# Hybrid encoder layer, attention stage: sample units that hold both key heads, a fourth probability buffer, and turns and values one round later

## The chip, the cores and the metric

The kernel runs on one core of a Trainium2 chip: a TensorE (PE) for matmuls, a VectorE (DVE), a ScalarE (ACT), a GpSimd (POOL), and DMA queues. The metric is the device time of one execution in microseconds, the median of three runs. A round, below, is one turn of the loop over attention units; a step is one piece of other matmul work put between them.

## The reference, cut to what matters

The layer runs over 1024 prompt rows and 8 samples of 16 new rows each. Ahead of the part shown stand a SwiGLU and one input projection, behind it an output projection and a second SwiGLU.

```python
def sink_attention(q, k, v, bias, sinks, mask=None):
    s = jnp.einsum('...qhgd,...khd->...hgqk', q, k) * (HEAD_DIM ** -0.5) + bias
    ...
    sink_col = jnp.broadcast_to(sink, s.shape[:-1] + (1,))
    p = jax.nn.softmax(jnp.concatenate([s, sink_col], axis=-1), axis=-1)[..., :-1]
    return jnp.einsum('...hgqk,...khd->...qhgd', p.astype(v.dtype), v)
...
attn, gm, state = mixer(q, k, v, u, vn)
merged = jax.nn.sigmoid(ga) * (attn @ w_ba) + jax.nn.sigmoid(gb) * (gm @ w_bg)
```

There are 16 query heads over 2 key heads, 64 wide. A prompt query sees its own chunk of 64 keys and the two before it; a sample's 16 queries see 128 cached keys and the 16 new ones.

## The kernel before

The rows stand in 9 tiles of 128: block 0 holds five prompt tiles, block 1 three prompt tiles and one tile of the 8 samples. Large matmuls are made of three (`mm3`, L254 to L256) from operands that are split into a high and a low part (L264 on ACT and L265 on DVE for activations, L157 and L160 for weights).

`attend` runs a block's attention. Its units are in a fixed order: for each of eight pairs of query heads every prompt tile of the block (40 units in block 0, 24 in block 1), and in block 1 then 16 sample units, one for each key head and sample. A unit has four stages. *Scores*: matmuls (L1202; L1270 and L1271 for samples), bias and row bound on DVE (L1205; L1273), exponentials on ACT (L1210; L1278), into a buffer `pb`. *Divide*: on DVE, sum, reciprocal and product in `pb` (L1225, or L1229 for the first tile; L1286 for samples). *Turn*: PE transposes the probabilities (L1237; L1291), and one copy takes them out of PSUM into `pt` (L1238, alternating between DVE and ACT; L1292 on DVE). *Values*: matmuls with the values (L1250; L1301), and after the last unit of a group a copy into `attn_f` (L1254; L1306).

Round u divides unit u-2, scores unit u, turns unit u-2 and forms the values of unit u-3; there are three prompt buffers `pb`. After the scores and after the turn come steps of `second()`, the filler: six matmuls of the gMLP branch (L254 to L256), 64 in all, ten of them ahead of the first unit, and a rate such that some stay over for the end. `strict` keeps each engine's instructions in the order in which they are written, so an instruction that waits holds up all behind it on its engine.

A sample unit uses 64 rows of the array for its scores and 64 columns for its values; GpSimd clears its part of `pb` (L1267). The last unit of a key head copies all its heads' outputs (L1306). When the attention is done, `put_split` splits each of the eight `attn_f` tiles (L264, L265), with a step of the filler in between, and `first()` multiplies them by `w_ba`; later on the same stretch the norms and transposes of the next stage follow (L332 on DVE, L435 on PE).

Of the kernel before, what the change touches and what calls it, by code (L numbers as in the profile page):

```python
# [27 lines left out]
P = 128  # L28
# [13 lines left out]
def tile_hybrid_layer(  # L42
# [827 lines left out]
    k_smp = place(52, P)  # L870
    q_smp = place(28).rearrange("p (b a q) -> p b a q", b=8, a=8)
    k_c = [place(32 + 2 * i, 512).rearrange("p (b j) -> p b j", b=4) for i in range(2)]
# [33 lines left out]
    class Block:  # L906
# [44 lines left out]
        def project(self, tasks):  # L951
# [3 lines left out]
            rs_t, rs_s = (place(kb, 512).rearrange("p (g i) -> p g i", g=4) for kb in (56, 58))  # L955
# [37 lines left out]
            def row_sums():  # L993

                ones = tmp(P)
                nc.gpsimd.memset(ones, 1.0)
                for out, wt in ((rs_t, ws_t), (rs_s, ws_s))[:1 + b]:
                    ps = bank().rearrange("p (g i) -> p g i", g=4)
                    nc.tensor.matmul(ps, ones, wt, start=True, stop=True)
                    nc.scalar.copy(out=out, in_=ps)  # L1000
# [75 lines left out]
            def done(g, m, c, j, v, in_place):  # L1076
# [33 lines left out]
                else:  # L1110
                    hp = slice(64 * (f // 4), 64 * (f // 4) + 64)
                    for e in range(2):
# [5 lines left out]
                        if n_pr < w:  # L1118
                            nc.scalar.activation(out=q_smp[hp, :, 2 * (f % 4) + e, :],
# [20 lines left out]
        def attention(self):  # L1140
            self.pb = [wide() for _ in range(3)]
# [6 lines left out]
            if self.b == 1:  # L1148
                units += [(self.sample_unit, (h, i)) for h in range(2) for i in range(8)]
            return units  # L1150

        def keys(self, h):
# [8 lines left out]
            if h == 1:  # L1161
                t = wr.tile([P, 2048], F32, tag="wr", name="wr")[:, :320 * self.n_k]
                nc.gpsimd.memset(t, 0.0)
                self.vz = t.rearrange("p (m c) -> p m c", c=320)
            nc.scalar.copy(out=self.vz[:, :, 64 + 128 * h:128 + 128 * h],
                           in_=v_t[:, self.t0:self.t0 + self.n_k, mine])
# [11 lines left out]
        def prompt_unit(self, p, mi, u):  # L1178
            m = self.tiles[mi]
            h = p // 4  # L1180
            pb = self.pb[u % 3]
# [50 lines left out]
            def turn():  # L1232
# [5 lines left out]
                (nc.vector.tensor_copy if u % 2 else nc.scalar.copy)(out=pt[:, a0:], in_=ps[:, a0:])  # L1238

            def values():  # L1240
# [6 lines left out]
                for a in range(a0, 2):  # L1247
                    for e in range(2):
                        at = 64 + 128 * h - 64 * e
                        nc.tensor.matmul(po[:, c0:c0 + P], self.vz[:, m - 1 - self.t0 + a, at:at + P],  # L1250
# [7 lines left out]
        def sample_unit(self, h, i, u):  # L1258
            hp = slice(64 * h, 64 * h + 64)
            pb = self.pb[u // 2 % 3][:, u % 2 * 256:u % 2 * 256 + 256]  # L1260
            pt = place(53, 768)[:, u % 3 * 256:u % 3 * 256 + 256].rearrange("p (a t) -> p a t", a=2)
            new = pb[:, P + 16 * i:P + 16 * i + 16]
            s = stat()
            sink = sink_s[:, h:h + 1]

            def scores():
                nc.gpsimd.memset(pb[:, P:256], 0.0)  # L1267
# [4 lines left out]
                sc = tmp(144)  # L1272
                nc.vector.tensor_tensor_reduce(out=sc, in0=ps[:, 0:144], in1=bs_s[:, h], scale=1.0,  # L1273
                                               scalar=nsink_s[:, h:h + 1], op0=ALU.add, op1=ALU.min,
                                               accum_out=s[:, 2:3])
                nm = s[:, 2:3]
                for v, src, c in ((pb[:, 0:P], sc[:, 0:P], 4), (new, sc[:, P:144], 5)):
                    nc.scalar.activation(out=v, in_=src, func=AF.Exp, bias=nm, scale=-1.0,  # L1278
                                         accum_out=s[:, c:c + 1])
                nc.scalar.activation(out=s[:, 6:7], in_=nm, func=AF.Exp, bias=sink)  # L1280

            def divide():
                nc.vector.scalar_tensor_tensor(out=s[:, 8:9], in0=s[:, 4:5], scalar=s[:, 5:6],
                                               in1=s[:, 6:7], op0=ALU.add, op1=ALU.add)
                nc.vector.reciprocal(out=s[:, 10:11], in_=s[:, 8:9])
                nc.vector.tensor_scalar(out=pb, in0=pb, scalar1=s[:, 10:11], scalar2=None, op0=ALU.mult)  # L1286

            def turn():
                ps = bank()[:, 0:256].rearrange("p (a t) -> p a t", a=2)
                for a in range(2):  # L1290
                    nc.tensor.transpose(ps[:, a, :], pb[:, a * P:(a + 1) * P], ident)  # L1291
                nc.vector.tensor_copy(out=pt, in_=ps)  # L1292

            def values():
                if i == 0:
                    self.out[8 + h] = bank()
                po = self.out[8 + h]
                rw = pt.rearrange("p a (g e q) -> p a g e q", g=4, e=2)
# [159 lines left out]
    dn = {}  # L1458
# [172 lines left out]
```

## Time and profile before

| | us |
|---|---|
| three runs | 2608.41, 2610.66, 2612.6 |
| median | 2610.66 |
| profiled execution, its own time | 2607.29 |
| its span, first to last instruction | 2605.3 |
| block 0's attention, in the span | 1104 to 1230 |
| block 1's attention | 1584 to 1720, its sample units from 1662 |

The span is 2 us under the profiled execution's time, which is 3.4 us under the median. The two attentions are a tenth of the span; nearly all of the rest is the projections and SwiGLUs. Times in the rows below are microseconds from the start of the span. In a timeline row the bracket at the end gives the idle time before the instruction and what ended it; PEclk is the granted TensorE clock as a share of 2.4 GHz.

### The profile page before, as it was taken

The numbers are of one execution on the slowest core, as the hardware profiler recorded it, in microseconds if no ns is written. First come the engines' busy times: TensorE is split into PE (matmuls) and PEld (weight loads), VectorE is DVE, ScalarE is ACT, GpSimd is POOL, SyncE is SP. The second block draws the span as 40 slices with busy tenths as digits, with TensorE's granted clock in tenths as the row PEclk, the third lists the DMA queues.
The fourth block names the chain that finished last, engine by engine and source line by source line (L and its number), as shares of the span: only waits on it lengthen the run. The fifth ranks groups of instructions, "written<-read, shape, count | busy, mean of one in ns | idle before, by whom it ended". The sixth has DMA issues, their size and how long they took to land.

```text
span 2605.3 us, 43435 instructions
## 1 busy us (share of the span) xinstructions
PE 2534.7 (97%) x16996; PEld 2375.2 (91%) x16996; DVE 1902.0 (73%) x3312; ACT 1392.3 (53%) x2589; POOL 197.3 (8%) x302
## 2 busy tenths in 40 slices
PE   6999999999999999999999998899999999999998
PEld 6999987999978999989989898897999987899986
DVE  6776664788877686687867877778876665688885
ACT  5444553555565555775446567535544464455552
POOL 1000000000210000101300201141000000000030
PEclk9999999999999999999999999989999999999999
DMA  4423322333443224423533443353322323433362
GB/s 123 95 84 97 114 80 96 129 115 101 162 146 116 80 92 134 129 89 128 174 110 98 142 149 112 108 193 132 114 82 90 98 81 109 126 102 111 128 210 81
DMA packets 222476, 303.35 MB, mean 116 GB/s; under 512 B 11848, under 2 KB 174000, under 8 KB 222272
## 3 DMA queue, kind: packets, MB, share of 16 engines
q1 hardware_dynamic: 183312, 212.36, 25.5%
q0 software_dynamic: 19584, 64.08, 8.1%
q10 hardware_dynamic: 19376, 24.15, 2.6%
q8 instruction: 133, 2.18, 0.4%
q14 instruction: 71, 0.58, 0.1%
HBM read 260.43 MB, written 40.11 MB: 115 GB/s over the span
## 4 chain that ended last, share of the span: by engine, by line
PE 88%; DVE 7%; DMA 2%; ACT 1%; issue 1%; ACTq 0%; DVEq 0%; SPq 0%
PE ps L254 27%; PE ps L256 27%; PE ps L255 27%; PE ps L1250 1%; DVE wl L160 1%; PE ps L435 1%; DMA wr<-in_ffn_w_up_dram 1%; PE ps L1237 1%; DMA wr<-in_w_in_dram 1%; DVE arena_r L265 1%; PE ps L1202 1%; DVE arena_r L1176 1%; PE ps L1050 0%; DMA y<-w 0%; DVE w L1205 0%
## 5 line engine op out<-in xcount | busy, mean ns | idle before, releaser
L254 PE MATMUL ps<-arena_r,wh 128*128 128x320 f32 (+1 forms) x4160 | 1243.8, 299 | 3.9 <-ACT arena_r L264 1.4
L256 PE MATMUL ps<-arena_r,wl 128*128 128x320 f32 (+1 forms) x4160 | 1229.2, 296 | 4.9 <-DVE wl L160 4.6
L255 PE MATMUL ps<-arena_r,wh 128*128 128x320 f32 (+1 forms) x4160 | 1230.5, 296 | 0.4 <-DVE arena_r L265 0.3
L254 PEld LDWEIGHTS ps<-arena_r,wh 128*128 128x128 f32 x4160 | 788.1, 189 | 7.0 <-ACT arena_r L264 1.7
L256 PEld LDWEIGHTS ps<-arena_r,wl 128*128 128x128 f32 x4160 | 786.9, 189 | 7.0 <-DVE wl L160 6.8
L255 PEld LDWEIGHTS ps<-arena_r,wh 128*128 128x128 f32 x4160 | 788.4, 190 | 1.9 <-DVE arena_r L265 0.8
L160 DVE TENSOR_TENSOR wl<-wr,wh 128x1024 fp32r<-128x1024 f32 x404 | 503.5, 1247 | 248.0 <-ACT wh L157 239.0
L157 ACT CAST wh<-wr 128x1024 fp32r<-128x1024 f32 x404 | 419.7, 1039 | 211.2 <-PE ps L255 168.8
L254 PE MATMUL ps<-wh,arena_r 128*128 128x512 f32 x936 | 375.7, 401 | 1.0 <-ACT arena_r L264 1.0
L256 PE MATMUL ps<-wh,arena_r 128*128 128x512 f32 x936 | 371.4, 397 | 0.4 <-DVE arena_r L265 0.4
L255 PE MATMUL ps<-wl,arena_r 128*128 128x512 f32 x936 | 369.3, 395 | 0.0
L264 ACT CAST arena_r<-arena 128x640 fp32r<-128x640 f32 (+4 forms) x260 | 167.8, 654 | 267.7 <-PE ps L255 224.4
L265 DVE TENSOR_TENSOR arena_r<-arena,arena_r 128x640 fp32r<-128x640 f32 (+4 forms) x260 | 197.2, 768 | 147.9 <-ACT arena_r L264 142.6
L256 PEld LDWEIGHTS ps<-wh,arena_r 128*128 128x128 f32 x936 | 176.1, 188 | 43.4 <-DVE arena_r L265 0.8
L255 PEld LDWEIGHTS ps<-wl,arena_r 128*128 128x128 f32 x936 | 176.3, 188 | 40.8
L254 PEld LDWEIGHTS ps<-wh,arena_r 128*128 128x128 f32 x936 | 176.2, 188 | 40.9 <-ACT arena_r L264 1.9
L541 DVE TENSOR_TENSOR t<-t,ps 128x320 f32<-128x320 f32 (+1 forms) x384 | 169.9, 448 | 44.9 <-PE ps L256 34.9
L160 DVE TENSOR_TENSOR wl<-arena,wh 128x1024 fp32r<-128x1024 f32 (+1 forms) x130 | 156.7, 1205 | 56.0 <-ACT wh L157 55.5
L545 ACT COPY t<-ps 128x320 f32<-128x320 f32 (+1 forms) x384 | 150.9, 395 | 80.8 <-PE ps L256 80.0
L157 ACT CAST wh<-arena 128x1024 fp32r<-128x1024 f32 (+1 forms) x130 | 134.6, 1036 | 109.0 <-PE ps L255 87.2
L597 ACT ACTIVATE t<-t 128x256 f32<-128x256 f32 (+1 forms) x129 | 57.2, 444 | 173.9 <-DVE t L541 173.8
L157 ACT CAST wh<-gn 128x1024 fp32r<-128x1024 f32 (+1 forms) x65 | 67.5, 1039 | 51.0 <-PE ps L255 42.1
(248 smaller groups left out, 2215.9 us busy)
## 6 DMA issues: line engine op xcount, KB each, us to landing
wr<-in_ffn_w_gate_dram SPq DMA_DIRECT2D x88, 512.0 KB, 4.0
wr<-in_ffn_w_up_dram SPq DMA_DIRECT2D x88, 512.0 KB, 5.0
wr<-in_w_in_dram SPq DMA_DIRECT2D x84, 512.0 KB, 4.8
wr<-in_ffn_w_down_dram SPq DMA_DIRECT2D x40, 1024.0 KB, 5.1
y<-w ACTq DMA_DIRECT2D x38, 256.0 KB, 3.4
arena<-x POOLq DMA_DIRECT2D x19, 512.0 KB, 4.5
arena<-y POOLq DMA_DIRECT2D x17, 512.0 KB, 4.9
x<-arena POOLq DMA_DIRECT2D x16, 512.0 KB, 3.0
```

The source lines that it names most:

```text
L157: nc.scalar.copy(out=self.hi, in_=self.src)
L160: nc.vector.tensor_tensor(out=self.lo, in0=self.src, in1=self.hi.bitcast(F32), op=ALU.subtract)
L254: nc.tensor.matmul(out, lh, rh, start=start, stop=False, skip_group_check=again)
L255: nc.tensor.matmul(out, lh, rl, start=False, stop=False, skip_group_check=again)
L256: nc.tensor.matmul(out, ll, rh, start=False, stop=stop, skip_group_check=again)
L264: nc.scalar.copy(out=hi, in_=src)
L265: nc.vector.tensor_tensor(out=lo, in0=src, in1=hi.bitcast(F32), op=ALU.subtract)
L435: nc.tensor.transpose(ps[:, c0:c0 + n], self.h[self.tiles[i]][p0:p0 + n, k * P:(k + 1) * P], ident[p0:p0 + n, p0:p0 + n])
L541: nc.vector.tensor_tensor(out=out, in0=a, in1=b, op=ALU.add)
L545: nc.scalar.copy(out=t, in_=ps)
L597: nc.scalar.activation(out=t, in_=v, func=AF.Silu)
L1176: nc.vector.tensor_tensor(out=t[other], in0=src, in1=t[mine].bitcast(F32), op=ALU.subtract)
```

## The change

A sample unit now holds both key heads. The queries of key head h lie in a tile of their own whose other 64 rows are zeros, so scores are matmuls over all 128 rows; the new values of each sample lie in the first 16 rows of a zeroed tile; eight units of four score matmuls, four transposes and two values matmuls of 256 columns replace sixteen. Every second unit copies two samples' outputs for all heads in four copies.

`pb` has four buffers (the fourth in the tile that also holds `vz`, the values among zeros, made narrower). Divide stays two rounds behind the scores; turn is three behind and values four. Three copies of four out of the turns go to ACT. The cached keys are copied by ACT in three instructions, where DVE needed eight.

```diff
@@ attention
-            self.pb = [wide() for _ in range(3)]
+            room = wr.tile([P, 2048], F32, tag="wr", name="wr")
+            self.vz = room[:, :256 * self.n_k + 64]
+            nc.gpsimd.memset(self.vz, 0.0)
+            self.pb = [wide() for _ in range(3)] + [room[:, 1536:2048]]
...
-                units += [(self.sample_unit, (h, i)) for h in range(2) for i in range(8)]
+                units += [(self.sample_unit, (i,)) for i in range(8)]
@@ prompt_unit, turn
-                (nc.vector.tensor_copy if u % 2 else nc.scalar.copy)(out=pt[:, a0:], in_=ps[:, a0:])
+                (nc.vector.tensor_copy if u % 4 == 3 else nc.scalar.copy)(out=pt[:, a0:], in_=ps[:, a0:])
@@ sample_unit
-                lq = q_smp[hp, i].rearrange("p a q -> p (a q)")
-                nc.tensor.matmul(ps[:, 0:P], lq, k_c[i // 4][hp, i % 4, :], start=True, stop=True)
-                nc.tensor.matmul(ps[:, P:P + 16], lq, k_smp[hp, 16 * i:16 * i + 16], start=True, stop=True)
+                if i < 4:
+                    nc.gpsimd.memset(pb[:, :, 144:256], 0.0)
...
+                for h in range(2):
+                    lq = q_smp[h][:, i].rearrange("p a q -> p (a q)")
+                    for c, k in ((0, k_c[:, i, :]), (P, k_smp[:, 16 * i:16 * i + 16])):
+                        nc.tensor.matmul(ps[:, 144 * h + c:144 * h + c + k.shape[-1]], lq, k, start=True, stop=True)
...
-                nc.vector.tensor_copy(out=pt, in_=ps)
+                nc.scalar.copy(out=pt, in_=ps)
...
-                for a, vv in ((0, v_c[:, i, hp]), (1, v_smp[:, hp])):
-                    for e in range(2):
-                        nc.tensor.matmul(po[64 * e:64 * e + 64, i * 64:(i + 1) * 64], vv,
-                                         rw[:, a, :, e, :], start=(a == 0), stop=(a == 1))
-                if i == 7:
...
+                for a, vv in ((0, v_c[:, i, :]), (1, v_new[i // 4][:, i % 4, :])):
+                    nc.tensor.matmul(po[:, i % 2 * 256:i % 2 * 256 + 256], vv, pt[:, a, :], start=a == 0, stop=a == 1)
+                if i % 2:
...
+                    for h in range(2):
+                        for e in range(2):
+                            (nc.vector.tensor_copy if e else nc.scalar.copy)(
...
@@ attend
-            lag = [[None] * 4] * 3
-            for u, (kind, arg) in enumerate(units + [(None, None)] * 3):
...
-                for i, f in enumerate((lag[1][1], cur[0], lag[1][2], lag[0][3])):
-                    if f:
-                        strict(f)
-                    if i in (1, 2):
+            late = {}
+            for u in range(len(units) + 4):
...
+                    for i, at in enumerate((0, 2, 3, 4)):
+                        late[u + at, i] = of[i]
+                for i in (1, 0, 2, 3):
+                    if (u, i) in late:
+                        strict(late.pop((u, i)))
+                    if i in (0, 2):
```

The order of PE's instructions at the start of block 0's attention, before: the scores of unit 2 (L1202), the turn of unit 0 (L1237, out of the buffer `w_10734`), a step (L254 to L256), the scores of unit 3:

```order
L1202 MATMUL ps_10898<-arena_r_88 128x192 x4
L1237 MATMUL ps_10908<-ident_89,w_10734 128x128 x2
L254 MATMUL ps_10834<-arena_r_88,wh_10700 128x320
L255 MATMUL ps_10834<-arena_r_88,wh_10700 128x320
L256 MATMUL ps_10834<-arena_r_88,wl_10701 128x320
L254 MATMUL ps_10835<-arena_r_88,wh_10700 128x320
L255 MATMUL ps_10835<-arena_r_88,wh_10700 128x320
L256 MATMUL ps_10835<-arena_r_88,wl_10701 128x320
L1202 MATMUL ps_10922<-arena_r_88 128x192 x4
```

The same place now, from the scores of unit 2 on (L1207 scores, L1242 the turn of unit 0, out of `w_10736`):

```order
L1207 MATMUL ps_10920<-arena_r_88 128x192 x4
L254 MATMUL ps_10838<-arena_r_88,wh_10700 128x320
L255 MATMUL ps_10838<-arena_r_88,wh_10700 128x320
L256 MATMUL ps_10838<-arena_r_88,wl_10701 128x320
L254 MATMUL ps_10839<-arena_r_88,wh_10700 128x320
L255 MATMUL ps_10839<-arena_r_88,wh_10700 128x320
L256 MATMUL ps_10839<-arena_r_88,wl_10701 128x320
L1242 MATMUL ps_10936<-ident_89,w_10736 128x128 x2
```

The turn of unit 0 stood right behind the scores of unit 2. Now a step, the scores of unit 3 and another step lie between them.

On DVE, the end of the sample units before (L1286 the last product, L1292 the last copy out of a turn, L1306 output copies, L265 the low parts of `attn_f`):

```order
L1286 TENSOR_SCALAR w_16287<-w_16287,st_17681 128x256
L1292 COPY arena_87<-ps_17744 128x256
L1306 COPY arena_87<-ps_17595 128x128
L265 TENSOR_TENSOR arena_r_88<-arena_87,arena_r_88 128x512
L1306 COPY arena_87<-ps_17595 128x128
L265 TENSOR_TENSOR arena_r_88<-arena_87,arena_r_88 128x512 x3
L1371 TENSOR_TENSOR t_17525<-t_17525,ps_17729 128x256
L1371 TENSOR_TENSOR t_17526<-t_17526,ps_17730 128x256
```

And now (L1292 is here the last product, L1314 the output copies, L1381 what L1371 was):

```order
L1292 TENSOR_TENSOR wr_16290<-wr_16290,st_17536 128x2x144
L1314 COPY arena_87<-ps_17600 64x4x32 x2
L1314 COPY arena_87<-ps_17642 64x4x32 x2
L265 TENSOR_TENSOR arena_r_88<-arena_87,arena_r_88 128x512 x4
L1381 TENSOR_TENSOR t_17408<-t_17408,ps_17592 128x256
L1381 TENSOR_TENSOR t_17409<-t_17409,ps_17593 128x256
L265 TENSOR_TENSOR arena_r_88<-arena_87,arena_r_88 128x512 x4
```

All eight splits now stand behind the last values; before, four of them stood in the middle of the sample units, behind the last unit of the first key head. Of the filler, three steps stay over behind block 1's last values where there were five.

## Rows read from the trace of the kernel before

**Rows 1.** The page: span, busy time of the engines, chain that ended last.

```profile
PE 2534.7 (97%) x16996; PEld 2375.2 (91%) x16996; DVE 1902.0 (73%) x3312; ACT 1392.3 (53%) x2589; POOL 197.3 (8%) x302
...
PE 88%; DVE 7%; DMA 2%; ACT 1%; issue 1%; ACTq 0%; DVEq 0%; SPq 0%
```

**Rows 2.** Waits of TensorE, 1090 to 1230: us in total, times, longest.

```profile
PE ps L1237 <- DVE w L1229: 6.6, 5, 2.3
PE ps L1237 <- DVE w L1225: 3.5, 4, 1.3
```

**Rows 3.** The same view, 1584 to 1725.

```profile
PE ps L1237 <- DVE w L1225: 9.5, 7, 2.6
PE ps L1291 <- DVE w L1286: 6.6, 4, 3.1
```

**Rows 4.** Busy time by stretch: us, then PE, PEld, DVE, ACT, POOL, PEclk.

```profile
1115.00:1220.00 105.00, 96.56 (x775) 94.37 (x773) 87.09 (x305) 71.62 (x232) 9.12 (x17) 1.00 0.30 96
```

**Rows 5.** TensorE's timeline at the start of both attentions: start us, us.

```profile
1109.74 0.43 PE L1237 MATMUL ps<-ident,w 128*128 128x128 f32 x2 [2.32 <-DVE w L1229]
...
1595.60 0.72 PE L1237 MATMUL ps<-ident,w 128*128 128x128 f32 x4 [2.63 <-DVE w L1225]
```

**Rows 6.** The same view, one prompt round of block 1.

```profile
1640.21 0.60 PE L1237 MATMUL ps<-ident,w 128*128 128x128 f32 x4
1640.64 1.06 PE L1250 MATMUL ps<-gn,wr 128*128 128x128 f32 x8
1641.46 0.67 PE L1202 MATMUL ps<-arena_r 128*128 128x192 f32 x4
```

**Rows 7.** Vector and scalar engines, 1115 to 1220, by form.

```profile
L1238 DVE COPY gn<-ps 128x512 f32<-128x512 f32 x14 | 9.6, 687 | 1.4 <-PE ps L1237 1.4
...
L1238 ACT COPY gn<-ps 128x512 f32<-128x512 f32 x15 | 8.5, 569 | 2.2 <-PE ps L1202 2.1
```

**Rows 8.** TensorE's timeline in the sample units.

```profile
1674.14 0.44 PE L1291 MATMUL ps<-ident,w 128*128 128x128 f32 x2
...
1675.21 0.34 PE L1301 MATMUL ps<-arena 128*64 128x64 f32 x4
...
1675.60 0.48 PE L1270 MATMUL ps<-arena 64*128 64x128 f32 x2
...
1676.14 0.44 PE L1291 MATMUL ps<-ident,w 128*128 128x128 f32 x2
...
1693.31 0.66 PE L1291 MATMUL ps<-ident,w 128*128 128x128 f32 x2 [3.14 <-DVE w L1286]
...
1695.81 0.79 PE L1270 MATMUL ps<-arena 64*128 64x128 f32 x2
...
1699.29 0.79 PE L1270 MATMUL ps<-arena 64*128 64x128 f32 x2
```

**Rows 9.** VectorE's timeline ahead of the third sample wait.

```profile
1690.62 0.69 DVE L265 TENSOR_TENSOR arena_r<-arena,arena_r 128x512 fp32r<-128x512 f32 x1 [0.36 <-ACT arena_r L264]
...
1692.82 0.35 DVE L1286 TENSOR_SCALAR w<-w,st 128x256 f32<-128x256 f32 x1
```

**Rows 10.** Busy time by stretch, columns as in group 4.

```profile
1596.00:1602.00 6.00, 6.00 (x41) 6.00 (x39) 3.50 (x16) 3.58 (x12) 0.00 (x0) 0.72 0.00 0
1694.00:1712.00 18.00, 18.00 (x103) 15.82 (x103) 7.51 (x31) 4.33 (x23) 3.93 (x8) 0.50 0.18 57
...
1730.00:1760.00 30.00, 30.00 (x259) 30.00 (x258) 29.13 (x71) 12.88 (x27) 21.87 (x29) 1.00 0.80 268
```

**Rows 11.** TensorE's and VectorE's timelines behind the last sample values.

```profile
1719.76 0.39 PE L254 MATMUL ps<-arena_r,wh 128*128 128x256 f32 x1
...
1720.17 0.29 DVE L1306 COPY arena<-ps 128x128 f32<-128x128 f32 x1 [3.69 <-ACT arena L1306]
1720.83 0.69 DVE L265 TENSOR_TENSOR arena_r<-arena,arena_r 128x512 fp32r<-128x512 f32 x1 [0.36 <-ACT arena_r L264]
```

**Rows 12.** Waits of TensorE, 1725 to 1800.

```profile
PE ps L435 <- DVE arena L332: 2.2, 1, 2.2
```

More of the change, by code (lines that the diff above doesn't have):

```diff
@@ L869, in tile_hybrid_layer @@
     bs_t = spw[:, 512:1024].rearrange("p (g i) -> p g i", g=4)
-    k_smp = place(52, P)
-    q_smp = place(28).rearrange("p (b a q) -> p b a q", b=8, a=8)
-    k_c = [place(32 + 2 * i, 512).rearrange("p (b j) -> p b j", b=4) for i in range(2)]
+    k_smp = place(59.5, P)
+    q_smp = [place(kb).rearrange("p (b a q) -> p b a q", b=8, a=8) for kb in (28, 52)]
+    k_c = place(32).rearrange("p (b j) -> p b j", b=8)
+    v_new = [place(kb, 512).rearrange("p (b c) -> p b c", b=4) for kb in (12, 8)]
     v_c = place(4).rearrange("p (b c) -> p b c", b=8)
@@ L954, in project @@
             vt = place(53.5, n * P)
-            rs_t, rs_s = (place(kb, 512).rearrange("p (g i) -> p g i", g=4) for kb in (56, 58))
+            rs_t = place(56, 512).rearrange("p (g i) -> p g i", g=4)
+            rs_s = place(58, 64).rearrange("p (g i) -> p g i", g=4)
             mv = stat()
@@ L999, in row_sums @@
                     nc.tensor.matmul(ps, ones, wt, start=True, stop=True)
-                    nc.scalar.copy(out=out, in_=ps)
+                    nc.scalar.copy(out=out, in_=ps[:, :, 0:out.shape[-1]])
             def ln_sums(i):
@@ L1111, in done @@
                     hp = slice(64 * (f // 4), 64 * (f // 4) + 64)
+                    if b == 1 and f % 4 == 0 and (c, j) == (0, 1):
+                        nc.gpsimd.memset(place(28 if f == 0 else 52)[64 - hp.start:128 - hp.start], 0.0)
                     for e in range(2):
@@ L1160, in keys @@
                 nc.vector.tensor_tensor(out=lo[rows], in0=src, in1=hi[mine].bitcast(F32), op=ALU.subtract)
[L1161 to L1166, printed above, removed]
+            v = self.vz[:, 64:].rearrange("p (m c) -> p m c", c=256)
+            nc.scalar.copy(out=v[:, :, 128 * h:128 * h + 64], in_=v_t[:, self.t0:self.t0 + self.n_k, mine])
         def queries(self, p, part):
@@ L1256, in prompt_unit, with sample_unit @@
             return scores, divide, turn, values
[L1258 to L1262, printed above, removed]
+        def sample_unit(self, i, u):
+            pb = self.pb[u % 4].rearrange("p (h j) -> p h j", h=2)
+            pt = self.pt[:, u % 2 * 512:u % 2 * 512 + 512].rearrange("p (a t) -> p a t", a=2)
@@ new lines, in scores @@
+                nm = s[:, 2:4]
+                for h in range(2):
+                    nc.vector.tensor_tensor_reduce(out=pb[:, h, 0:144], in0=ps[:, 144 * h:144 * h + 144],
+                                                   in1=bs_s[:, h], scale=1.0, scalar=nsink_s[:, h:h + 1],
+                                                   op0=ALU.add, op1=ALU.min, accum_out=nm[:, h:h + 1])
+                nc.vector.tensor_tensor(out=s[:, 12:14], in0=nm, in1=sink_s, op=ALU.add)
+                for h in range(2):
+                    nc.scalar.activation(out=pb[:, h, 0:144], in_=pb[:, h, 0:144], func=AF.Exp, scale=-1.0,
+                                         bias=nm[:, h:h + 1], accum_out=s[:, 4 + h:5 + h])
@@ L1290, in turn @@
                 for a in range(2):
-                    nc.tensor.transpose(ps[:, a, :], pb[:, a * P:(a + 1) * P], ident)
-                nc.vector.tensor_copy(out=pt, in_=ps)
+                    for h in range(2):
+                        nc.tensor.transpose(ps[:, a, h * P:(h + 1) * P], pb[:, h, a * P:(a + 1) * P], ident)
+                nc.scalar.copy(out=pt, in_=ps)
             def values():
-                if i == 0:
-                    self.out[8 + h] = bank()
-                po = self.out[8 + h]
@@ L1298, in values @@
[L1298 to L1308 removed]
+                if i % 2 == 0:
+                    self.out[8 + i // 2] = bank()
@@ L1316, in load @@
             def load():
+                for t in v_new:
+                    nc.gpsimd.memset(t, 0.0)
+                for i in range(8):
+                    nc.gpsimd.dma_start(out=v_new[i // 4][0:16, i % 4, :], in_=v_smp[16 * i:16 * i + 16, :])
                 nc.gpsimd.dma_start(out=v_c, in_=cache_v[0].rearrange("b t h d -> t b (h d)"))
@@ L1327, in f @@
                         nc.tensor.transpose(ps[:, i * P:(i + 1) * P], raw[q][:, i, :], ident)
-                    for i in range(b0, b1):
-                        nc.vector.tensor_copy(out=k_c[i // 4][:, i % 4, :],
-                                              in_=ps[:, (i - b0) * P:(i - b0 + 1) * P])
+                    nc.scalar.copy(out=k_c[:, b0:b1], in_=ps[:, :(b1 - b0) * P].rearrange("p (b j) -> p b j", j=P))
                 return f
@@ L1397, in step @@
                         return
+            raws["n"] = 2
             units = self.attention()
```

51 lines of the change are left out of this document (22 added, 29 removed).

## The prediction

> **What bounds the kernel.** I read the page first. PE is busy 97% of the span, and the chain that ended last is PE for 88% and DVE for 7% [rows 1]. So only three things can move the time: PE's work, PE's waits, and PE's clock. Next I read PE's waits in the two attentions. In block 0 the turns (L1237) wait 6.6 and 3.5 us for the divide of the unit that they transpose (L1229, L1225), 10.1 us in nine waits [rows 2]. In block 1 the prompt turns wait 9.5 us in seven and the sample turns (L1291) 6.6 us in four [rows 3]. The reader should see that it is always the same pair: a turn, and the divide on DVE just ahead of it. The longest is 3.1 us.
>
> Why the divides are late is shown by the busy times. From 1115 to 1220 PE has 96.6 us of work in 105, DVE 87.1 and ACT 71.6 [rows 4]: DVE is fast enough on average, so it is late only in bunches. One bunch stands ahead of the longest wait: splits of the first key head's outputs (L265), from 1690.62 on at 0.69 us each, lie on DVE in front of the divide of 1692.82, for which the turn of 1693.31 has waited 3.14 us [rows 8, 9].
>
> Last I read the clock. It is 1.00 in block 0 even behind a 2.32 us wait [rows 4, 5]. Behind the 2.63 us wait at the start of block 1 it averages 0.72 over 6 us, and from 1694 to 1712, behind the 3.14 us wait, it is 0.50, that is 1.2 GHz, while PE is never idle [rows 5, 8, 10].
>
> **Part by part.** *Turn and values one round later, a fourth buffer.* A prompt round takes about 2.5 us: turn 0.43 and values 0.82 from start to start; the scores' row says 0.67, but a turn whose row says 0.60 is followed after 0.43, and in that ratio it is 0.48 [rows 6]; and a step of six matmuls, 0.70 (30.0 us over 259 matmuls, 0.116 each [rows 10]). A turn now has one round more before it needs its divide. The longest waits are 2.3 and 2.6 us [rows 2, 3], the others shorter than a round, so nearly all should vanish unless DVE is later still. Three copies of four out of the turns go to ACT: a quarter of 36 copies leaves DVE in that stretch, 9 x 0.69 = 6.2 us of its 87.1, and costs ACT 9 x 0.57 = 5.1 on 71.6 [rows 4, 7]; both stay below PE. PE's own instructions are the same. I leave 1.5 us of waits in block 0 and 1.0 in block 1: gains of 8.6 and 8.5 us. The bounds are none gone and all gone, 0 and 10.1, 0 and 9.5. With no wait of 2.63 us, the clock should hold at 1596. At 0.72 over 6 us, 0.56 of them are at half speed, 3.4 us, of which half comes back: 1.7 us (bounds 0 and 1.7).
>
> *Sample units.* A round of before takes 2.00 us at full clock (1674.14 to 1676.14), of which about 0.70 is a step: 1.30 a unit, 20.8 us for 16 [rows 8, 10]. A new unit has four transposes as a prompt unit has, 0.43. Its two values matmuls move 256 columns each, as many as the four of 128 of a prompt unit: 0.82 [rows 6]. Its scores the trace does not show in this form. One pair with 64 rows took 0.54 (1675.60 to 1676.14) [rows 8], so two pairs are 1.08 by that row; a prompt unit's scores, 0.5, are the lower end. I take 0.85, nearer the upper one, whose columns are the same. That gives 2.1 us a unit and 16.8 for eight, a gain of 4.0 us (bounds 2.2 and 6.8).
>
> One thing speaks against it. The values of two old units, with 64 columns of the array each, take 2 x 0.39 = 0.78 us (1675.21 to 1675.60) [rows 8], hardly less than the 0.82 that I put for a new one. The Trainium skill, "TensorEngine Tiling (Array Packing)", Overview and Key Properties, has it that matmuls on separate 64-column parts of the array can run beside each other, up to twice as fast, which the full array gives up. By that page the values of a new unit could cost up to twice the old ones, and the sum would be some 6 us smaller; it is the rival of the full array below. I go by the prompt unit's row, which is a full-array matmul of the same type.
>
> *Sample waits.* The splits that caused the longest wait move behind the last values, since each output copy now writes all heads. DVE's work for the samples falls: one copy and one product fewer per pair, and the copies out of the turns go to ACT. The 6.6 us should fall to about 0.5: gain 6.1 (bounds 0, 6.6). *Sample clock.* A sample round took 3.48 us at half clock (1695.81 to 1699.29) against 2.00 at full: of 18 us at 0.50, 18 x (1 - 2.00/3.48) = 7.7 us come back if the clock stays up [rows 8, 10] (bounds 0, 7.7).
>
> *Behind the samples.* This costs. Before, the last values ended at 1719.76; the last four splits followed from 1720.83, and five steps (3.5 us) covered them [rows 11]. Now three steps stay over, 2.1 us (two were done earlier; this alone costs nothing). Four output copies of about 0.29 in a row, ACT's part of the first split (put as long as L265) and the first L265 make 1.2 + 0.7 + 0.7 = 2.6, 0.5 more than is covered; the other L265 come one per 0.69, as fast as PE uses them, but between the fourth and the fifth stand two sums of 256 columns, which at half an L265 are 0.7. With signals I put PE's stall at 1.4 us. DVE is busy 29.1 of 30 us from 1730 to 1760 [rows 10] and has four more splits to do here, 2.8 us, with nothing to spare; this work ends in L332, for which PE already waits 2.2 us [rows 12]. So this wait grows by 2.8. Together +4.2 us (bounds 0, and 8 x 0.69 + 1.4 = 6.9).
>
> *At nothing:* the eight loads of new values, GpSimd's memsets (the zeros in queries and values are written in the projection and ahead of the units, and POOL is busy 8% [rows 1]), the cached keys' copies on ACT (fewer and off DVE), and `vz` taken earlier. The added wait is GpSimd's: clearing `pb` for the first four sample units stands behind its loads, and the transposes on PE wait for it. If a load holds it up, each of four turns waits; by the longest wait of a turn so far, 3.1 us [rows 3], that is up to 12 us. I take nothing, since the buffers' last readers are three rounds old by then.
>
> **The sum.** -8.6 - 8.5 - 1.7 - 4.0 - 6.1 - 7.7 + 4.2 = -32.4 us. From 2607.3 for the profiled execution that gives 2574.9; its own time is 3.4 below the median of 2610.7, so I forecast a median of 2578.3, say 2578.
>
> **Rivals.** *The clock falls in the sample stretch all the same* (0.13). For it: it stayed at 0.50 for 18 us without a gap [rows 10], so what runs there did not bring it back. Against: in block 0 it held at 1.00 through rounds with four transposes each, as a new sample round has [rows 4]. The 7.7 us are not gained: 2586. The Trainium skill, "TensorE: Matmul & The Clock Gate", Part 4, says that transposes do not count as activity in the same way; block 0's 1.00 is against that deciding here.
>
> *Lateness moves on* (0.15): DVE's bunches are longer than a round, half of the 23.2 us of waits stay. For it: DVE 83% busy. 2590.
>
> *The change doesn't do what it says* (0.04): the turns wait in the new place as long as in the old, because DVE falls behind steadily rather than in bunches. All 23.2 us stay, 2602. Against: DVE has 18 us free in 105 [rows 4], so it does not fall behind for good.
>
> *Slower* (0.03): the clock falls at the first wait of block 1 and stays at 1.2 GHz through its attention. A round at half clock costs 3.48 for 2.00, 0.74 us more for each us of work, so from 44 us of such work on the gain of 32.4 is gone; all 130 us would cost 96 and end 64 above before, at 2674. Against: behind the 2.63 us wait it came back within 6 us [rows 10].
>
> *The full array costs more* (0.05): a new unit's values take twice the 0.78 us of two old ones, 1.56 for 0.82, 5.9 us in eight units: 2584. For it: the four records of one old group stand close together, 0.39 us for all eight of a unit [rows 8]. Against: the prompt's 0.82 for the same columns [rows 6].
>
> *More than forecast* (0.13): scores at the lower bound and the splits covered: 2571. The forecast itself has 0.47.
>
> **Range and chances.** The range takes in the forecast, the better case, the clock, the lateness and the full array (0.93), with 5 us below the better case for the waits' better bounds, and leaves out the two cases at 2602 and above: 2566 to 2594. A measurement here can tell about 0.2%, 5 us. Faster 0.95, same 0.02, slower 0.03.
>
> **What would show it.** In the changed profile, waits of the turns for DVE near 1.5, 1.0 and 0.5 us in the three stretches; PEclk 1.00 through the samples; the sample units' matmuls at 2.1 us a unit; PE idle about 1.4 us behind the last values, and the wait before L332's reader near 5 us. The prediction is wrong if turns still wait several us, if the waits reappear at values or scores, if a turn waits for GpSimd, or if PE's gap at the end of the attention is several times what I put.

## The result and the profile after

The changed kernel takes 2575.8 us (median of four runs, 2568.1 to 2579.4) against 2611.3 for the kernel before beside it: a ratio of 0.9864, interval 0.9851 to 0.9877, or 35.5 us less. The forecast was 2578, range 2566 to 2594. The profiled execution has a span of 2574.6 us, 30.7 less than before, though PE's first matmul waited 11.8 us for a load in it and 8.2 before, which has nothing to do with the change. A second set of runs of the same kernel gave 0.9860 (0.9844 to 0.9875).

To see where the time went, cut the span at instructions that both kernels have. The view of one line gives, after count and durations, the first and the last start. Before:

```profile
L1202 PE MATMUL ps<-arena_r x160: 192/276/338, 1104.2 to 1215.3; 128*128 128x192 f32 x128, 128*128 128x64 f32 x16, 128*128 128x128 f32 x16
...
L1250 PE MATMUL ps<-gn,wr x288: 271/275/376, 1112.7 to 1226.7; 128*128 128x128 f32 x144
...
L1202 PE MATMUL ps<-arena_r x96: 251/274/417, 1590.1 to 1659.9; 128*128 128x192 f32 x96
...
L1270 PE MATMUL ps<-arena x32: 271/373/580, 1662.2 to 1706.9; 64*128 64x128 f32 x32
...
L1301 PE MATMUL ps<-arena x64: 222/270/370, 1673.2 to 1719.3; 128*64 128x64 f32 x64
...
L435 PE MATMUL ps<-ident,arena x48: 270/273/331, 1779.9 to 1818.5; 128*128 128x128 f32 x32, 64*128 64x64 f32 x16
```

After (L1207 scores, L1255 values, L1276 and L1307 the samples' scores and values):

```profile
L1207 PE MATMUL ps<-arena_r x160: 191/276/337, 1107.3 to 1209.1; 128*128 128x192 f32 x128, 128*128 128x64 f32 x16, 128*128 128x128 f32 x16
...
L1255 PE MATMUL ps<-gn,wr x288: 272/275/377, 1116.5 to 1220.2; 128*128 128x128 f32 x144
...
L1207 PE MATMUL ps<-arena_r x96: 252/274/337, 1583.8 to 1647.5; 128*128 128x192 f32 x96
...
L1276 PE MATMUL ps<-arena x64: 182/268/356, 1649.7 to 1672.9; 128*128 128x128 f32 x32, 128*128 128x16 f32 x32
...
L1307 PE MATMUL ps<-gn,arena x32: 377/378/382, 1664.8 to 1684.6; 128*128 128x256 f32 x32
...
L435 PE MATMUL ps<-ident,arena x48: 270/273/475, 1747.3 to 1787.1; 128*128 128x128 f32 x32, 64*128 64x64 f32 x16
```

| stretch on PE | before, us | after, us | change |
|---|---|---|---|
| block 0: first scores to last values | 122.5 | 112.9 | -9.6 |
| block 1: first scores to first sample scores | 72.1 | 65.9 | -6.2 |
| first sample scores to last sample values | 57.1 | 34.9 | -22.2 |
| last sample values to first L435 | 60.6 | 62.7 | +2.1 |

Each entry is a difference of two starts above, as 1226.7 - 1104.2 = 122.5. The rest of the -30.7 is +3.1 ahead of block 0's attention and +2.1 in the other stretches; most of the latter lies behind the first L435. Steps have moved too: by the count of L254, the first matmul of each half of a step, the prompt units of block 1 now hold seven more of them (68 such matmuls for 54) and the sample units five fewer. At 0.70 us a step, the second row is about -11.1 without them and the third about -18.7. Together block 1's attention went from 129.2 to 100.8 us although two more steps of 0.70 stand in it.

The waits of PE, in the stretches that answer to [rows 2, 3 and 12] (us in total, times, longest; 1090 to 1236, 1560 to 1695, 1695 to 1780):

```profile
PE ps L1255 <- ACT gn L1243: 1.8, 2, 1.3
...
PE ps L1255 <- issue: 1.3, 1, 1.3
PE ps L1255 <- ACT gn L1243: 0.5, 1, 0.5
PE ps L1299 <- DVE wr L1292: 0.5, 1, 0.5
...
PE ps L435 <- DVE arena L332: 3.8, 1, 3.8
PE ps L255 <- DVE wl L160: 1.2, 1, 1.2
```

No prompt turn waits for a divide any more: 19.6 us are gone, and of the samples' 6.6 there are 0.5. In their place values wait for ACT's copies, 2.3 us, and once for nothing that the profile shows, 1.3. L435 waits 1.6 us longer for L332, and 1.2 us is new.

Busy time by stretch, columns as in [rows 4]:

```profile
1118.00:1209.00 91.00, 90.41 (x737) 89.60 (x736) 76.42 (x278) 70.33 (x227) 9.64 (x18) 1.00 0.33 107
...
1650.00:1684.00 34.00, 33.49 (x270) 32.52 (x269) 20.20 (x81) 17.54 (x60) 4.86 (x11) 1.00 0.39 123
1747.00:1756.00 9.00, 8.72 (x30) 6.21 (x30) 6.31 (x10) 3.76 (x7) 0.00 (x0) 0.63 0.37 119
```

PE is busy 99% in block 0's middle, where it was 92% [rows 4], and 98% in the samples, at full clock; from 1694 to 1712 the kernel before had 0.50 [rows 10]. DVE's share in block 0's middle is 84%, and was 83%: not its load has changed but the moment at which its work is due. The last row stands behind the first L435: after the wait of 3.8 us the clock averages 0.63 over 9 us. The same stretch in the kernel before, behind its wait of 2.2 us, and in the profile of the second set of runs of the changed kernel, again behind 3.8 us:

```profile
1780.00:1789.00 9.00, 9.00 (x36) 6.50 (x37) 7.01 (x11) 3.81 (x7) 0.00 (x0) 0.81 0.39 119
1746.00:1755.00 9.00, 8.45 (x33) 6.32 (x34) 7.35 (x12) 4.05 (x7) 0.00 (x0) 0.81 0.38 118
```

So the wait is longer in both profiles of the changed kernel, but the longer stay at the low clock in one only; that part is no sure price of the change.

### The profile page after: what moved, and what is told of

The parts are those of the page before. It is cut to its first block, busy times and chain, and to the rows that moved or that the text cites. A ratio compares the mean times of both kernels' runs of the same rounds, so it can differ in the third digit from the quotient of the medians.

```text
span 2574.6 us, 43142 instructions
## 1 busy us (share of the span) xinstructions
PE 2520.0 (98%) x16900; PEld 2364.1 (92%) x16900; DVE 1883.1 (73%) x3260; ACT 1395.7 (54%) x2580; POOL 202.1 (8%) x306
## 4 chain that ended last, share of the span: by engine, by line
PE 88%; DVE 4%; DMA 3%; ACT 2%; issue 1%; POOL 0%; ACTq 0%; DVEq 0%; SPq 0%; POOLq 0%
PE ps L254 27%; PE ps L256 27%; PE ps L255 27%; PE ps L1255 2%; PE ps L435 1%; DVE wl L160 1%; DMA wr<-in_ffn_w_up_dram 1%; PE ps L1242 1%; DMA wr<-in_w_in_dram 1%; PE ps L1207 1%; DMA y<-w 1%; PE ps L1054 0%; DVE arena_r L265 0%; PE ps L992 0%; ACT wh L157 0%
## 5 line engine op out<-in xcount | busy, mean ns | idle before, releaser
L254 PE MATMUL ps<-arena_r,wh 128*128 128x320 f32 (+1 forms) x4160 | 1239.3, 298 | 4.1 <-ACT arena_r L264 1.4
L256 PE MATMUL ps<-arena_r,wl 128*128 128x320 f32 (+1 forms) x4160 | 1225.4, 295 | 6.2 <-DVE wl L160 5.9
L255 PE MATMUL ps<-arena_r,wh 128*128 128x320 f32 (+1 forms) x4160 | 1226.7, 295 | 0.5 <-DVE arena_r L265 0.3
L256 PEld LDWEIGHTS ps<-arena_r,wl 128*128 128x128 f32 x4160 | 783.1, 188 | 8.5 <-DVE wl L160 8.3
L254 PEld LDWEIGHTS ps<-arena_r,wh 128*128 128x128 f32 x4160 | 784.1, 189 | 6.9 <-ACT wh L157 1.8
L160 DVE TENSOR_TENSOR wl<-wr,wh 128x1024 fp32r<-128x1024 f32 x404 | 503.8, 1248 | 251.2 <-ACT wh L157 242.0
L254 PE MATMUL ps<-wh,arena_r 128*128 128x512 f32 x936 | 376.0, 402 | 1.6 <-ACT arena_r L264 1.6
L256 PE MATMUL ps<-wh,arena_r 128*128 128x512 f32 x936 | 371.1, 397 | 1.0 <-DVE arena_r L265 1.0
L265 DVE TENSOR_TENSOR arena_r<-arena,arena_r 128x640 fp32r<-128x640 f32 (+4 forms) x260 | 194.6, 759 | 147.9 <-ACT arena_r L264 143.0
L256 PEld LDWEIGHTS ps<-wh,arena_r 128*128 128x128 f32 x936 | 176.1, 188 | 44.6 <-DVE arena_r L265 1.9
L254 PEld LDWEIGHTS ps<-wh,arena_r 128*128 128x128 f32 x936 | 176.3, 188 | 41.9 <-ACT arena_r L264 2.8
L541 DVE TENSOR_TENSOR t<-t,ps 128x320 f32<-128x320 f32 (+1 forms) x384 | 169.9, 448 | 44.7 <-PE ps L256 34.6
L160 DVE TENSOR_TENSOR wl<-arena,wh 128x1024 fp32r<-128x1024 f32 (+1 forms) x130 | 156.7, 1205 | 54.8 <-ACT wh L157 54.3
L597 ACT ACTIVATE t<-t 128x256 f32<-128x256 f32 (+1 forms) x129 | 57.2, 443 | 175.2 <-DVE t L541 175.1
L199 DVE TENSOR_TENSOR arena<-wr 128x1024 f32<-128x1024 f32 (+1 forms) x65 | 78.4, 1207 | 26.2 <-DMA wr<-in_w_in_dram 12.3
```

Of the source, the lines that this page charges most:

```text
L160: nc.vector.tensor_tensor(out=self.lo, in0=self.src, in1=self.hi.bitcast(F32), op=ALU.subtract)
L199: nc.vector.tensor_tensor(out=out, in0=x, in1=y, op=op)
L254: nc.tensor.matmul(out, lh, rh, start=start, stop=False, skip_group_check=again)
L255: nc.tensor.matmul(out, lh, rl, start=False, stop=False, skip_group_check=again)
L256: nc.tensor.matmul(out, ll, rh, start=False, stop=stop, skip_group_check=again)
L265: nc.vector.tensor_tensor(out=lo, in0=src, in1=hi.bitcast(F32), op=ALU.subtract)
```

## The experiments

All ratios are to the kernel before, run beside each. Stage times in the table come from the same view of first and last starts, one profile each. The kernels with eight sample units have the steps moved as above, so the columns for block 1's prompt units and for the samples compare directly only among kernels with as many sample units.

| kernel | ratio, interval | block 0 | block 1 prompt | samples | to L435 |
|---|---|---|---|---|---|
| before | 1 | 122.5 | 72.1 | 57.1 | 60.6 |
| changed | 0.9864 (0.9851 to 0.9877) | 112.9 | 65.9 | 34.9 | 62.7 |
| late turns only | 0.9891 (0.9876 to 0.9907) | 115.2 | 64.4 | 44.7 | 60.0 |
| merged samples, old distances | 0.9935 (0.9922 to 0.9947) | 120.2 | 73.3 | 37.3 | 62.2 |
| copies alternating | 0.9873 (0.9859 to 0.9887) | 115.2 | 66.4 | 35.0 | 62.7 |
| before, outputs last | 0.9956 (0.9942 to 0.9970) | 124.1 | 72.0 | 45.6 | 61.2 |
| late turns only, DVE stall | 0.9941 (0.9923 to 0.9960) | 115.1 | 64.4 | 57.2 | 60.2 |
| changed, short DVE stall | 0.9868 (0.9844 to 0.9893) | 112.9 | 65.8 | 37.8 | 62.7 |
| changed, long DVE stall | 0.9898 (0.9880 to 0.9916) | 112.9 | 65.7 | 42.6 | 62.7 |
| three buffers | 1.0127 (1.0106 to 1.0148) | 155.8 | 91.1 | 37.4 | 62.7 |
| three buffers, turn first | 0.9866 (0.9849 to 0.9884) | 116.0 | 65.9 | 34.9 | 62.7 |
| split in the samples | 0.9864 (0.9843 to 0.9885) | 112.8 | 65.8 | 38.7 | 59.9 |
| split spread | 0.9872 (0.9854 to 0.9891) | 112.9 | 70.3 | 34.9 | 62.1 |

**Late turns alone.** The kernel before with the new loop of `attend` and four buffers, old sample units, copies alternating.

```diff
-            lag = [[None] * 4] * 3
+            late = {}
...
+                    for i, at in enumerate((0, 2, 3, 4)):
+                        late[u + at, i] = of[i]
```

> The kernel before with the fourth buffer, turns three and values four rounds late, and nothing else: sample units one key head each, copies alternating as before. My theory: lateness of turns is what removes the prompt waits, so block 0 gains about 9 us (first scores to last values 122.5 to about 113) and block 1's prompt units about 10 with the clock; the sample waits go too, and if the clock then holds, 8 more: about 2583, ratio 0.989. Rival, that the lighter DVE and the merged sample units do it: prompt waits stay near 19 us, about 2605, ratio above 0.996.

Measured 2581.6 us, 0.9891: the theory's figure. The waits of the turns in block 0, and in block 1 with the samples (L1236 and L1290 turns, L1249 values):

```profile
PE ps L1249 <- ACT gn L1237: 2.1, 3, 1.3
PE ps L1236 <- DVE wr L1224: 1.6, 1, 1.6
...
PE ps L1249 <- ACT gn L1237: 2.5, 3, 2.1
...
PE ps L1290 <- DVE w L1285: 1.4, 2, 1.2
```

Of 26.2 us of turn waits [rows 2, 3] 3.0 are left; values wait 4.6 us for ACT's copies. Block 0 takes 115.2 us, not the 113 that the theory gave, and the prompt units gain 7.7 us rather than 10. The rival falls: the waits go although units and copies are the old ones.

**Merged samples alone.** The changed kernel with the old distances.

```diff
-                    for i, at in enumerate((0, 2, 3, 4)):
+                    for i, at in enumerate((0, 2, 2, 3)):
```

> The changed kernel with the old distances: turns two and values three rounds late. My theory: prompt waits of 10 us in block 0 and 9 in block 1 come back in good part (a little fewer, since fewer copies are on DVE), the sample gains stay: about 2594, ratio 0.9935. Rival, that moving copies off DVE and merging carry it: about 2580, ratio below 0.989.

Measured 2594.1 us, 0.9935. The turns wait again, 8.4 us in block 0, 4.3 in block 1's prompt units and 3.2 in the samples in these lines (other lines of the same views add 0.3, 1.4 and 1.1):

```profile
PE ps L1242 <- DVE w L1234: 6.3, 5, 2.3
PE ps L1242 <- DVE w L1230: 2.1, 3, 1.2
...
PE ps L1242 <- DVE w L1230: 4.3, 5, 2.2
...
PE ps L1299 <- DVE wr L1292: 3.2, 2, 2.6
```

Lateness and merging are worth 28 and 17 us alone and 35 together. They overlap in the samples' longest wait and the low clock behind it, which either one removes.

**Copies alternating.**

```diff
-                (nc.vector.tensor_copy if u % 4 == 3 else nc.scalar.copy)(out=pt[:, a0:], in_=ps[:, a0:])
+                (nc.vector.tensor_copy if u % 2 else nc.scalar.copy)(out=pt[:, a0:], in_=ps[:, a0:])
```

> The changed kernel with the prompt copies out of the turns alternating between DVE and ACT as before. My theory: DVE has room once turns are late, so no change beyond 2 us, ratio 0.986 to 0.988; the values that now wait for ACT's copies (2.3 us in all) wait less. Rival, that taking a quarter of the copies off DVE matters: 5 us or more slower than the changed kernel, ratio above 0.9885.

Measured 0.9873, inside the interval of the changed kernel. Block 0 is 2.3 us longer in the profile, 1.7 of it a turn that waits for DVE; the values' wait for ACT is not less:

```profile
PE ps L1255 <- ACT gn L1243: 2.1, 3, 1.3
PE ps L1242 <- DVE wr L1230: 1.7, 1, 1.7
```

So moving a quarter of the copies is worth some 2 us. Both kernels with alternating copies have 115.2 us in block 0, but the whole times can't tell this from nothing.

**The clock in the old samples.** The kernel before, with both key heads' sample outputs copied at the end, so that no split stands in front of a divide.

```diff
-                if i == 7:
-                    src = po.rearrange("p (b g q) -> p g b q", b=8, g=4)
-                    for g in range(4):
+                if i == 7 and h == 1:
+                    for hh in range(2):
+                        src = self.out[8 + hh].rearrange("p (b g q) -> p g b q", b=8, g=4)
...
```

> The kernel before, with the first key head's sample outputs copied at the end together with the second's, so that its four splits no longer stand in front of a divide in the middle of the sample units. My theory: the 3.1 us wait goes, and with it the 18 us at 1.2 GHz, for 3 + 8 us, less 4 us for eight splits behind the last values: about 2604, ratio 0.997. Rival, that the old sample units themselves hold the clock low: the low clock stays, no gain or a loss of 1 to 3 us, ratio 1.000 or more.

Measured 0.9956, 11.5 us faster, from this edit alone. The stretch that had the low clock now reads, by busy time:

```profile
1690.00:1714.00 24.00, 20.52 (x203) 17.98 (x198) 18.71 (x66) 10.98 (x47) 5.66 (x14) 1.00 0.44 142
```

The sample turns still wait in it:

```profile
PE ps L1291 <- DVE w L1286: 3.9, 3, 2.4
```

PEclk is 1.00 throughout, and the samples take 45.6 us for 57.1. Of the 11.5 us, 2.7 are waits (3.9 for the 6.6 of [rows 3]); the other 8.8 I put down to the clock. The old sample units do not make the clock fall by themselves: in the samples it is 1.00 until the last of these waits, of 2.4 us, and falls only behind it, to 0.63 and 0.52 between 1714 and 1718. Eight splits behind the last values cost 0.6 us here, with five steps to cover them, not the 4 that I had put.

**What brings the clock back.** Two kernels with needless copies on DVE ahead of one sample divide: the late-turns kernel with its old units, and the changed kernel. The first, 18 copies ahead of unit 6:

```diff
+                if (h, i) == (0, 6):
+                    for _ in range(18):
+                        nc.vector.tensor_copy(out=pb, in_=pb)
```

> The kernel with late turns and the old sample units (measured at 0.9891), with 18 needless copies on DVE ahead of the divide of sample unit 6, some 7 us, so that one turn waits some 4 us. Theory A: the clock falls and stays at 1.2 GHz for 15 to 20 us, as in the kernel before: 4 + 7 us, about 2593, ratio 0.993. Theory B gives the same here; that the clock's stay does not hang on the work at all: it comes back within 7 us, about 2588, ratio 0.991.

Measured 0.9941, 13 us over the same kernel without the stall. The turn that waited, on PE's timeline, and the busy time behind it:

```profile
1682.57 0.41 PE L1293 MATMUL ps<-ident,w 128*128 128x128 f32 x2 [3.23 <-DVE w L1288]
```

```profile
1690.00:1700.00 10.00, 10.00 (x59) 8.75 (x58) 6.35 (x23) 5.01 (x19) 0.20 (x1) 0.50 0.07 23
1700.00:1706.00 6.00, 6.00 (x37) 5.07 (x37) 2.49 (x10) 1.57 (x10) 3.17 (x6) 0.50 0.31 104
1706.00:1710.00 4.00, 4.00 (x37) 3.66 (x36) 3.50 (x8) 1.05 (x1) 0.55 (x2) 0.78 0.85 285
```

PE is busy 16.0 of 16 us at 0.50, as in the kernel before. The mean granted clock of a whole execution agrees: 0.992 or 0.993 in all four with this stall, 0.994 to 0.996 in the four without. The new units, with the same 18 copies ahead of unit 3 and then with 32:

> The changed kernel with 18 needless copies on DVE (each some 0.4 us, about 7 us) ahead of the divide of sample unit 3, so that one turn waits some 4 us in the middle of the new sample units. Theory A, that a wait of over 3 us lets the clock fall and the old units' work kept it low: here it falls too, but comes back within 7 us, so about 4 + 2 us, 2582, ratio 0.9888. Theory B, that the work of any sample unit keeps it low once it has fallen: 15 us or more at 1.2 GHz, 4 + 7 us, 2587, ratio 0.9907.

Measured 0.9868: the longest wait was 1.4 us, the later turn hid the rest, and the clock did not fall. This run tells nothing of the theories.

> The changed kernel with 32 needless copies on DVE (0.31 us each as measured, 9.9 us) ahead of the divide of sample unit 3; 18 copies gave waits of 1.4 us at most and no fall of the clock. The longest wait should now be 4 to 6 us. Theory A, that the new sample units' work brings the clock back while the old units' work does not: 1.2 GHz for 3.4 or 6.8 us, 2584 or so, ratio 0.9895. Theory B, that the work of any sample unit keeps it low once it has fallen: 15 us or more at 1.2 GHz, 2589, ratio 0.9915.

Measured 0.9898. PE's timeline, and the busy time behind the wait:

```profile
1677.47 1.09 PE L1302 MATMUL ps<-ident,wr 128*128 128x128 f32 x4 [6.24 <-DVE wr L1295]
```

```profile
1677.00:1679.00 2.00, 1.53 (x8) 1.56 (x9) 1.06 (x6) 1.35 (x6) 0.00 (x0) 0.50 0.00 0
1679.00:1681.00 2.00, 2.00 (x10) 1.83 (x10) 1.28 (x5) 0.54 (x3) 0.00 (x0) 0.66 0.00 0
1681.00:1683.00 2.00, 2.00 (x20) 2.00 (x19) 1.86 (x12) 1.45 (x6) 1.06 (x2) 1.00 0.00 0
```

The wait is twice as long as in the old units, the clock fell during it and is 0.50 at its end, but 3.5 us later it is 1.00. The interval of the ratio takes in the figures of both theories, so it is the trace that speaks for A: after a wait of 6.2 us the new units had full clock back within 3.5 us, after one of 3.2 us the old units ran 16 us and more at half of it. It is one profile each, beside the kernel before with its 18 us, and what ran in the new units until the clock was back was one turn, one step and values, no scores yet.

What of the old units does this (64 rows, 64 columns, or the small matmuls) was not taken apart. The traces hold a hint: in the kernel before and in the stalled one the clock came back 5 to 6 us after the last old scores had started (1707.07 and 1702.33), while turns, steps and the values over 64 columns still ran; it is 0.78 from 1712 to 1714 before, and 0.78 from 1706 to 1710 in the rows above. So the values alone did not hold it down. That leaves the scores, or the larger share of steps in rounds without scores, and no run tells these apart.

**The fourth buffer.** The changed kernel with `pb = self.pb[u % 3]` in the prompt units. Here unit u+3's scores overwrite the buffer ahead of unit u's turn, so the turn takes the later unit's probabilities.

> The changed kernel with three probability buffers for the prompt units, turns still three rounds late, so that a unit's scores on DVE must wait for a turn that PE does later in the same round. My theory: the fourth buffer is what makes the later turn free; DVE loses up to 1 us of each of 64 rounds, and with 83% of work it becomes the bound: 10 to 40 us slower than the changed kernel, ratio 0.990 to 1.001. Rival: the wait lies in DVE's free time, within 3 us of the changed kernel, ratio 0.985 to 0.9875.

Measured 1.0127, 34 us slower than the kernel before. The wait is not the one that I expected: the turn waits for exponentials of its own round (L1215 on ACT), 32 times in block 0:

```profile
PE ps L1242 <- ACT w L1215: 24.8, 32, 2.6
```

The run shows the price of a turn without any lateness, not that of the missing buffer. So the buffer was tried again with an order in which three are enough:

```diff
-                for i in (1, 0, 2, 3):
+                for i in (1, 2, 0, 3):
```

> The changed kernel with three probability buffers for the prompt units and the turn of unit u-3 ahead of the scores of unit u in its round, so that the buffer is free when they are written; steps stand behind the turn and the scores. A turn then has some 1.5 us more than before the change, not a whole round. My theory: most waits are shorter than that, so 0 to 6 us slower than the changed kernel, ratio 0.986 to 0.989, the fourth buffer being worth little by itself. Rival: DVE's bunches need the whole round, and the scores now wait for DVE behind late turns: 10 us or more slower, ratio above 0.990.

Measured 0.9866, the same as the changed kernel; block 0 is 3.1 us longer in the profile, the turns wait for DVE a little again:

```profile
PE ps L1242 <- DVE w L1230: 1.9, 1, 1.9
PE ps L1242 <- DVE w L1234: 1.6, 2, 1.4
```

With the order changed in this way, the fourth buffer is worth some 3 us by the profile, which the whole times can't tell from nothing; a turn that comes later is what counts.

**The splits behind the samples.** Two kernels split the prompt columns of `attn_f` early and only the 128 sample columns behind the last values.

```diff
+                if i < 8:
+                    self.part_split(P_ORDER[i], slice(0, self.n_p * P))
...
-                put_split(*self.attn[p], self.attn_f[p])
+                self.part_split(p, last)
```

> The changed kernel with each head pair's prompt columns split during the sample units, one pair a round, and only the 128 sample columns split behind the last values. My theory: eight splits of 512 columns behind the last values are what makes DVE late for L332 (PE waits 3.8 us there, and 6.8 us at 1.2 GHz follow); with 128 columns DVE has 8 x 0.4 = 3 us less there, the wait falls below 2 us and the clock piece shrinks: 2 to 5 us faster than the changed kernel, ratio 0.9845 to 0.9858. Rival: the splits make divides late in the sample units instead, no gain or a loss, ratio 0.9865 or more.

Measured 0.9864, no gain. The stretch to L435 falls by 2.8 us to 59.9, as forecast, though the wait for L332 stays at 2.7, not below 2, and the clock behind it is no higher (0.62 over 9 us). But the samples grow by 3.8: the last turns (L1301) and values (L1309) wait.

```profile
PE ps L435 <- DVE arena L332: 2.7, 1, 2.7
PE ps L1301 <- DVE w L1294: 1.6, 1, 1.6
...
PE ps L1309 <- ACT gn L1302: 1.1, 2, 0.7
```

> The changed kernel with the prompt columns of six head pairs split during block 1's prompt units (two pairs later) and of the last two during the sample units, and only the 128 sample columns split behind the last values. The same split in the sample units alone (ratio 0.9864) won 2.8 us behind the last values and lost 3.8 us to waits in the last sample rounds. My theory: spread over rounds with more slack, the loss goes and the 2.8 us stay: about 2573, 2 to 4 us faster than the changed kernel run beside it. Rival: DVE's or ACT's bunches in the prompt units grow past a round's slack, and as much is lost there, no difference or slower.

Measured 0.9872; the changed kernel beside it had 0.9860.

> The changed kernel itself, to stand beside the others on the same chip: 0.985 to 0.988.

In this kernel the last pair's split stands in the round of its last values, but ahead of them, and so takes old columns; the work is the same. The loss moved to the prompt units, 70.3 us for 65.9, where scores wait for splits (L265):

```profile
PE ps L1207 <- DVE arena_r L265: 2.2, 2, 1.4
...
PE ps L435 <- DVE arena L332: 1.4, 1, 1.4
```

L435's wait fell from 3.8 to 1.4, so DVE's splits are what makes L332 late. But DVE's and ACT's time for them has to be paid in one place or another, and no version tried here beats the changed kernel.

## Why the prediction was right

The mechanism and nearly all terms held. *Waits in block 0*: -8.6 forecast, -9.6 measured. The late-turns kernel had 7.3 of it with nothing else changed; the other 2.3 came with the copies given to ACT, for which the prediction had no gain of their own, since the kernel with these alternating has 115.2 us as well. *Block 1's attention*: waits, clock at 1596, sample work, sample waits and sample clock came to -28.0; measured 28.4 less with two more steps in it, or -29.8. Both pieces of low clock are gone, and a third with them that the prediction left out. Behind the last sample wait of before, of 1.99 us, the clock fell again:

```profile
1716.00:1720.00 4.00, 4.00 (x31) 3.32 (x30) 0.42 (x1) 0.12 (x1) 1.67 (x4) 0.57 0.96 304
```

At 0.57 over 4 us, 3.4 us are at half speed, by the prediction's own rate about 1.5 us more to come back: most of the 1.8 us by which this part was put too low.

*The sample unit's price* was well put. On PE's timeline of the changed kernel:

```profile
1668.44 1.03 PE L1307 MATMUL ps<-gn,arena 128*128 128x256 f32 x4
1669.31 0.96 PE L1276 MATMUL ps<-arena 128*128 128x128 f32 x8
1670.12 0.63 PE L1299 MATMUL ps<-ident,wr 128*128 128x128 f32 x4
1670.51 0.37 PE L254 MATMUL ps<-arena_r,wh 128*128 128x256 f32 x1
```

Values take 0.87 us, scores 0.81 and the turn 0.39, 2.07 a unit where I had 0.82, 0.85 and 0.43, for two old ones of 1.30. The rival of the full array, by which values would have cost 1.56, fell: two old units had 0.78. The Trainium skill, "TensorEngine Tiling (Array Packing)", Overview, gives packing on half the columns up to twice the speed. In this kernel the trace shows far less: the packed values took 0.78 us and those on the full array 0.87, for as many columns.

*Behind the samples* I had put +4.2, 1.4 of it a stall of PE and 2.8 a later L332. The sum was near: +2.1, or +3.5 without the two steps that moved. The rest of the span behind the first L435 grew by 1.9 us, from 825.4 to 827.3, in the profile with 0.63, and by 0.6 in the second one with 0.81. The split of the sum was not. On DVE's timeline the splits follow one another as I had them:

```profile
1686.43 2.50 DVE L265 TENSOR_TENSOR arena_r<-arena,arena_r 128x512 fp32r<-128x512 f32 x4 [0.23 <-ACT arena_r L264]
1688.95 0.75 DVE L1381 TENSOR_TENSOR t<-t,ps 128x256 f32<-128x256 f32 x2
1689.62 2.50 DVE L265 TENSOR_TENSOR arena_r<-arena,arena_r 128x512 fp32r<-128x512 f32 x4
```

but PE has no wait for them: the first four are done by 1688.93, and high parts, from ACT, let four matmuls run ahead. What is late is paid further on. DVE's queue stays full to the end of the stretch, by busy time:

```profile
1695.00:1746.00 51.00, 47.26 (x360) 44.53 (x359) 49.43 (x130) 24.71 (x53) 31.47 (x40) 1.00 0.75 250
```

There PE waits 1.2 us for the split of a weight (L160), and 1.6 us more than before for L332 at its end. The step that was mis-sized is the stall of PE, 1.4 us, which did not come; 1.2 us was lost to L160 instead, and L332's part is 1.6 for 2.8.

*The rivals.* The clock did not fall in the samples, lateness did not move on by more than the 2.3 us that values wait for ACT, and nothing slower took place. That the clock would be a rival of the new units at all was a wrong reading on my side: I counted 18 us at 0.50 for it, and the stall runs tie this to the old units.

The summed change was 32.4 us, and the medians differ by 35.5. The stretches from block 0's first scores to the first L435 account for this: they sum to -35.9, each a little better than its forecast (by 1.0, 1.8 and 0.7 us). The profiled execution shows only 30.7 of it, since +3.1 lie ahead of the attention, where PE waits 3.6 us longer for its first load, and +2.1 elsewhere. The medians' 35.5 lies near the -35.9, but the four runs of the changed kernel differ by 11.3 us.

## What to carry to other kernels

In block 0's middle one engine was 92% busy and another one 83%, and the first waited for the second in pieces of up to 2.3 us [rows 2, 4]. The cure here was to consume the result a round later: lateness alone gave 28 us, and moving a quarter of the copies off the second engine some 2 us, not clear of noise. Look at what stands in front of the late instruction on its engine: here four splits that were not urgent, in front of a divide that was, cost 11.5 us with what the clock made of it. And a consumer may be put ahead of the next producer in the round rather than given another buffer.

## What the runs showed of the hardware

In these runs TensorE stayed at 1.2 GHz for longer or shorter according to what it ran behind the wait. With the old sample units (matmuls over 64 rows or 64 columns of the array between steps) PE was busy 16.0 of 16 us at a granted clock of 0.50 after a wait of 3.23 us; with the new units over the whole array the clock was back at 1.00 within 3.5 us of the end of a wait of 6.24 us. A busy PE alone did not bring it back there; in both kernels with old units it came back once their scores were done.

Nor did the length of a wait alone decide whether the clock fell. In the kernel before it was 1.00 from 1108 to 1115, around the wait of 2.32 us [rows 5], and fell behind the one of 1.99 us at the end of the samples. Behind the same wait of 3.8 us for L332, two profiles of the changed kernel have 0.63 and 0.81 over 9 us.

In block 0's middle, where a round of 2.5 us has a turn of 0.43, the granted clock is 1.00 before and after the change. The Trainium skill, "TensorE: Matmul & The Clock Gate", Part 4, has it that transposes do not count as activity in the same way; no run here shows that they cost the clock.
